# Reciprocal roots in two VectorE steps in PSUM, and the heads' rotation after their root

## The chip, the cores and the metric

The kernel runs on one core of a Trainium2 chip. The metric is the device time of one execution in microseconds, the median of several runs; lower is better.

The core has a matrix engine (TensorE, in the profile PE for its matmuls and PEld for its weight loads), an elementwise engine (VectorE, DVE), an engine for functions (ScalarE, ACT), a general engine (GpSimd, POOL) and a queue that issues transfers (SyncE, SP). Tensors lie in SBUF or in PSUM, where TensorE writes its products. Each engine works through its own instructions in a fixed order and waits for semaphores of the others.

## What is computed

The reference runs two transformer blocks, each of two layers, on 512 tokens with 1024 features, in float32. The first block mixes tokens in three ways (a Fourier transform, a gated recurrence, a latent attention) and also reads a context of 256 tokens. The second block has a grouped attention of 8 query heads over 2 key heads and a dilated attention of 3 groups of 4 heads. Every layer ends in an MLP with a squared ReLU. What matters here are the reciprocal roots, in every norm, and the norm and rotation of the heads in the second block:

```python
def rms(x, g):
    x32 = x.astype(jnp.float32)
    y = x32 * lax.rsqrt(jnp.mean(x32 * x32, axis=-1, keepdims=True) + EPS)
    return (y * g.astype(jnp.float32)).astype(x.dtype)

def apply_rope_2(x, cos, sin):
    x1, x2 = jnp.split(x32, 2, axis=-1)
    return jnp.concatenate([x1 * c - x2 * s, x2 * c + x1 * s], axis=-1).astype(x.dtype)

# for each group of the dilated attention, and in the same way for the grouped one
qs.append(apply_rope_2(rms(qb, q_norm_b[l, g]), *seq_cs))
kss.append(apply_rope_2(rms(kb, k_norm_b[l, g]), *seq_cs))
```

## The kernel before

Features lie on the partitions and tokens on the free axis, so the stream x is eight tiles of 128 x 512. Products take float32 operands in two parts, a high and a low one: a unit of weights (8 tiles of 128 x 128) is fetched by SyncE's queue, cut into its parts by ScalarE (line 120) and GpSimd (line 121), and used in 24 matmuls of 512 columns (lines 143, 144 and 146; `mm3`). TensorE runs one unit after the other through all stages, and the other engines serve it.

The program is written as Python loops and generators, which interleave their steps (`weave`); a planner then orders the instructions of each engine by their place in the program and by its own estimate of when each can start, and adds the semaphores. So the order on an engine is not exactly that of the text, and it is fixed before the run.

`rsqrt` (lines 152 to 161) makes (scale * mean + eps) ** -0.5 of a sum in PSUM. ScalarE takes a logarithm (line 156) and an exponential (line 157); then a Newton step follows on VectorE in four instructions (lines 158 to 161): one reads the sum from PSUM, three work in SBUF. It is called 64 times in an execution: by the norms of the stream (`norm_r`), by the latents' norms (`rms_small`), by the recurrence's output (`mlstm_out`) and 34 times, on 128 x 512, by `head_block`.

`head_block` (lines 1119 to 1146) takes a unit's product, the queries or keys of two heads, and normalizes and rotates it. ScalarE copies the product out of PSUM and squares it (lines 1127 to 1129), VectorE makes the low part of the squares (line 1130). The rest waits in a list, `pending`, until the next unit of products has been issued (`flush` in `project`): TensorE sums the squares over each head into a `pt` bank of PSUM (lines 1134 and 1135), `rsqrt` makes the root, and VectorE shuffles the block (line 1139), multiplies with the gains and the sine or cosine tables (lines 1140 and 1141), adds (line 1142) and multiplies with the root (line 1143). PSUM has two `pt` banks; the transposes of the attentions' softmax (lines 1184 and 1232), the value blocks and the norms take from the same two.

`mixers2` (line 1252) runs the second block's attention: a key block, four query blocks (`qa`), a `flush`, and then the six blocks of `dil_proj(0)` woven with the grouped attention (`gqa`) and the six of `dil_proj(1)` woven with the first half of the dilated attention (`dilated`). In the first layer the first block's final norm is woven in too (`finish`).

Of the kernel before, what the change touches and what calls it, by code (L numbers as in the profile page):

```python
# [10 lines left out]
F32 = mybir.dt.float32  # L11
# [6 lines left out]
EPS = 1e-6  # L18
# [5 lines left out]
HALVES = (slice(0, 256), slice(256, 512))  # L24


class Cols:
    """Per-feature vectors, side by side as columns of one array."""
# [33 lines left out]
def cut(t, H, classes):  # L62
    """The tokens H of t, whose order may be that of the classes modulo 4."""
    return by_classes(t)[:, :, H.start // 4:H.stop // 4] if classes else t[:, H]


def weave(a, b, na, nb):
    """Steps of two generators, in turn: nb of b spread over na of a."""
# [12 lines left out]
class Stream:  # L81
    """Tokens whose features lie on the partitions: x, eight blocks of [128, n]."""
# [6 lines left out]
class Kernel:  # L89
# [33 lines left out]
    def weights(self, src, nk, nm=128, dve=False, extra=None):  # L123
        """A unit of the weights, in two parts; extra: the tag of a third place."""
# [11 lines left out]
    def mm3(self, out, w, xs, ks=None, wide=False):  # L136
        """out += w[:, i].T @ xs[i], each operand in two parts."""
# [9 lines left out]
        if not wide:  # L147
            # short products leave the low part of the weights more time
            for i, (xh, xl) in enumerate(xs):
                nc.tensor.matmul(out, lo[:, ks[i] if ks else i], xh, start=False, stop=i == n - 1)  # L150

    def rsqrt(self, out, mean_ps, scale, tmp, eps=EPS):
        """out = (scale * mean + eps) ** -0.5; the tables' result takes a Newton step to float32's accuracy."""
        nc = self.nc
        p = mean_ps.shape[0]
        nc.scalar.activation(out=out, in_=mean_ps, func=AF.Ln, scale=scale, bias=(self.eps if eps == EPS else self.eps2)[:p])
        nc.scalar.activation(out=out, in_=out, func=AF.Exp, scale=-0.5)
        nc.vector.tensor_scalar(out=tmp, in0=mean_ps, scalar1=-0.5 * scale, scalar2=-0.5 * eps, op0=ALU.mult, op1=ALU.add)
        nc.vector.tensor_tensor(out=tmp, in0=tmp, in1=out, op=ALU.mult)  # L159
        nc.vector.tensor_tensor(out=tmp, in0=tmp, in1=out, op=ALU.mult)  # L160
        nc.vector.scalar_tensor_tensor(out=out, in0=tmp, scalar=1.5, in1=out, op0=ALU.add, op1=ALU.mult)

    def sigmoid(self, out, x, t=None):
        """out = 1 / (1 + exp(-x)), with no exponential of a positive number; with t, x is read at once."""
# [49 lines left out]
    def mod_cols(self, mod, ps, bias, at, nb, nv):  # L214
        """Rows 32 q + v of the sums to columns: mod[:, v, at + nb q + b]."""
# [12 lines left out]
    def gemv_now(self, r, src, out, tag, start, stop):  # L228
        """Round r of the first modulation, for both vectors, in steps, with TensorE's four column groups."""
# [17 lines left out]
    def gemvs_now(self, mod, rounds, src, bias):  # L247
        """Up to four rounds, in one tile of sums."""
# [7 lines left out]
    def gemv_later(self, mod, r, src, bias, vs):  # L256
        """A round of a modulation, in steps, on VectorE."""
# [31 lines left out]
    def until(self, n):  # L289
        """The first n of the modulations' later rounds are done."""  # L290
# [3 lines left out]
    def gain(self, name, g, sc):  # L294
        a = self.const.tile([128, 8], F32, name=name)
        self.nc.vector.scalar_tensor_tensor(out=a, in0=sc, scalar=1.0, in1=g, op0=ALU.add, op1=ALU.mult)
        return a

# [1 line left out]
    def norm_tag(self, s, H):  # L300
        """Where the tiles of a norm lie: by halves, some are held for long, and have a place of their own."""
# [4 lines left out]
    def norm_add(self, s, k, w=None, H=None):  # L306
        """Takes block k of s.x into the sum of squares, weighted with a column of w; H: of some tokens."""
# [33 lines left out]
    def scaled(self, out, x, a, r, classes):  # L341
        """out = a r x; classes: the tokens of out lie in classes modulo 4."""
# [14 lines left out]
    def norm_mod(self, s, a, sh, r=None, classes=False):  # L357
        """The normed and modulated blocks of s.x, each in two parts."""
# [20 lines left out]
    def norm_steps(self, s, a, sh, weighted=False, classes=False):  # L379
        """norm_mod by halves of the tokens; the first half's norm_r is done."""  # L380
# [1293 lines left out]
```

## Time and profile before

Three runs took 3576.43, 3580.7 and 3587.28 us; their median is 3580.7 us. The page and every row below are of one profiled execution, of which the page gives the span, from the first instruction to the last.

| | us | share of the span |
|---|---|---|
| span of the profiled execution | 3586.3 | |
| TensorE matmuls busy | 3376.2 | 94% |
| TensorE weight loads busy (beside the matmuls) | 2646.2 | 74% |
| VectorE busy | 2140.4 | 60% |
| ScalarE busy | 1456.4 | 41% |
| GpSimd busy | 1147.3 | 32% |

The span lies 5.6 us above the median of the runs and inside their spread. Busy shares are means over stages that differ; the second block's layers have their mixers at about 1960 to 2300 us and 2790 to 3110 us. The granted clock is the share of TensorE's full speed that it was allowed in a stretch; it has two levels, 2.4 GHz (1.00) and 1.2 GHz (0.50).

### The profile page before, as it was taken

What the parts mean: (1) busy time and instruction counts of PE and PEld (TensorE: products, weight loads), DVE (VectorE), ACT (ScalarE), POOL (GpSimd) and SP (SyncE); (2) the same over time, 40 slices, a digit from 0 to 9 for tenths busy, and PEclk for the clock granted to TensorE, in tenths of its full rate; (3) what the DMA queues carried; (4) which work ended last, traced back from release to release, by engine and by line L of the source; (5) the groups of instructions that cost most, each with busy time, mean ns of one, the idle gap of its engine ahead of it and who ended that gap; (6) DMA issues with size and microseconds to landing.
All of it is one profiled execution on the core that took longest, in us unless ns stands there. A gap on an engine that the chain in (4) does not pass through costs nothing.

```text
span 3586.3 us, 47387 instructions
## 1 busy us (share of the span) xinstructions
PE 3376.2 (94%) x18518; PEld 2646.2 (74%) x18518; DVE 2140.4 (60%) x3006; ACT 1456.4 (41%) x2551; POOL 1147.3 (32%) x539
## 2 busy tenths in 40 slices
PE   6989998999997889989998899999999899999999
PEld 4666667888886666678777656888888757788887
DVE  5764357564457863385667977466645867454333
ACT  4545444121233554343223555543223455643222
POOL 1222033222324321144443312344444312343443
PEclk8999999999999989999999999999999999999999
DMA  7731122343335422034453101224542101222232
GB/s 268 258 117 59 32 75 89 106 130 106 106 112 179 142 68 63 21 110 144 164 173 128 65 31 52 81 91 150 170 138 94 59 30 53 75 96 88 95 100 94
DMA packets 146706, 377.88 MB, mean 105 GB/s; under 512 B 16737, under 2 KB 32690, under 8 KB 146354
## 3 DMA queue, kind: packets, MB, share of 16 engines
q1 hardware_dynamic: 146482, 374.85, 31.9%
q8 instruction: 146, 2.39, 0.3%
q14 instruction: 78, 0.64, 0.1%
HBM read 363.48 MB, written 9.86 MB: 104 GB/s over the span
## 4 chain that ended last, share of the span: by engine, by line
PE 51%; DVE 10%; issue 2%; ACT 2%; DMA 0%; POOL 0%; DVEq 0%; ACTq 0%; POOLq 0%
PE pm L143 13%; PE pm L144 13%; PE pm L146 12%; PE p L968 1%; DVE y L346 1%; PE pt L1184 1%; PE p L1166 1%; PE pt L143 1%; PE pt L144 1%; PE pm L938 1%; PE pt L1192 1%; DVE hraw L1141 1%; PE pt L1232 1%; DVE hv L159 1%; PE pm L150 1%
## 5 line engine op out<-in xcount | busy, mean ns | idle before, releaser
L121 POOL TENSOR_TENSOR wlo<-raw,whi 128x1024 fp32r<-128x1024 f32 (+2 forms) x461 | 1096.7, 2380 | 2260.7 <-ACT whi L120 2118.7
L120 ACT CAST whi<-raw 128x1024 fp32r<-128x1024 f32 (+2 forms) x468 | 477.0, 1019 | 1208.5 <-PE pm L144 987.5
L143 PE MATMUL pm<-h,whi 128*128 128x512 f32 (+1 forms) x2312 | 856.0, 379 | 9.8 <-ACT raw_s L541 3.9
L144 PE MATMUL pm<-h,whi 128*128 128x512 f32 (+1 forms) x2312 | 844.7, 373 | 0.7 <-DVE h L374 0.7
L146 PE MATMUL pm<-h,wlo 128*128 128x512 f32 x1816 | 722.4, 398 | 3.3 <-POOL wlo L121 3.3
L143 PEld LDWEIGHTS pm<-h,whi 128*128 128x128 f32 x2312 | 443.3, 192 | 104.7 <-issue 19.0
L144 PEld LDWEIGHTS pm<-h,whi 128*128 128x128 f32 x2312 | 441.9, 191 | 77.0 <-issue 5.7
L143 PE MATMUL pm<-hid,whi 128*128 128x512 f32 (+1 forms) x1280 | 462.2, 370 | 21.8 <-DVE x L445 17.5
L144 PE MATMUL pm<-hid,whi 128*128 128x512 f32 (+1 forms) x1280 | 459.9, 368 | 3.9 <-DVE hid L513 3.9
L269 DVE SCALAR_TENSOR_TENSOR ga<-g,svec,ga 128x512 f32<-128x512 f32 x280 | 337.2, 1211 | 151.5 <-DMA g<-in_w_mod 149.9
L146 PEld LDWEIGHTS pm<-h,wlo 128*128 128x128 f32 x1816 | 346.8, 191 | 80.1 <-POOL wlo L121 5.8
L146 PE MATMUL pm<-hid,wlo 128*128 128x512 f32 x976 | 384.6, 394 | 1.7 <-POOL wlo L121 1.7
L509 DVE TENSOR_TENSOR relu<-relu 128x512 f32<-128x512 f32 (+1 forms) x169 | 255.6, 1513 | 190.1 <-ACT relu L507 189.9
L445 DVE SCALAR_TENSOR_TENSOR x<-pm,mod,x 128x512 f32<-128x512 f32 (+1 forms) x184 | 125.3, 684 | 357.9 <-PE pm L146 349.4
L143 PEld LDWEIGHTS pm<-hid,whi 128*128 128x128 f32 x1280 | 244.2, 191 | 65.7 <-issue 19.6
L144 PEld LDWEIGHTS pm<-hid,whi 128*128 128x128 f32 x1280 | 243.9, 191 | 45.4 <-DVE hid L513 6.9
L146 PEld LDWEIGHTS pm<-hid,wlo 128*128 128x128 f32 x976 | 185.6, 190 | 41.5 <-POOL wlo L121 3.0
L507 ACT ACTIVATE relu<-pm 128x512 f32<-128x512 f32 (+1 forms) x160 | 85.5, 534 | 144.9 <-PE pm L146 135.7
L513 DVE TENSOR_TENSOR hid<-relu,hid 128x512 fp32r<-128x512 f32 (+1 forms) x169 | 110.1, 651 | 14.5 <-ACT hid L512 0.4
L951 ACT ACTIVATE D<-pt,cc 128x256 f32<-128x256 f32 (+1 forms) x176 | 75.0, 448 | 99.5 <-PE pt L945 59.2
L325 DVE TENSOR_TENSOR acc<-acc,sq 128x256 f32<-128x256 f32 (+1 forms) x96 | 86.7, 903 | 25.2 <-ACT sq L317 22.7
L373 ACT ACTIVATE h<-y,mod 128x256 fp32r<-128x256 f32 (+1 forms) x136 | 67.7, 528 | 81.9 <-DVE y L346 81.6
(398 smaller groups left out, 4898.6 us busy)
## 6 DMA issues: line engine op xcount, KB each, us to landing
g<-in_w_mod SPq DMA_DIRECT2D x352, 256.0 KB, 3.0
raw<-in_w_in SPq DMA_DIRECT2D x142, 512.0 KB, 3.5
raw<-in_w_down SPq DMA_DIRECT2D x136, 512.0 KB, 3.5
raw<-in_w_up SPq DMA_DIRECT2D x128, 512.0 KB, 3.5
raw<-in_w_out SPq DMA_DIRECT2D x24, 512.0 KB, 3.5
g<-in_w_mod SPq DMA_DIRECT2D x16, 512.0 KB, 7.5
raw<-in_w_out SPq DMA_DIRECT2D x16, 384.0 KB, 3.3
raw<-in_w_br SPq DMA_DIRECT2D x16, 384.0 KB, 3.0
```

The costliest lines, as they stand in the source:

```text
L120: nc.scalar.copy(out=hi, in_=src)
L121: (eng or nc.vector).tensor_tensor(out=lo, in0=src, in1=hi.bitcast(F32), op=ALU.subtract)
L143: nc.tensor.matmul(out, hi[:, k], xh, start=i == 0, stop=False)
L144: nc.tensor.matmul(out, hi[:, k], xl, start=False, stop=False)
L146: nc.tensor.matmul(out, lo[:, k], xh, start=False, stop=i == n - 1)
L269: nc.vector.scalar_tensor_tensor(out=a, in0=g, scalar=sk, in1=a, op0=ALU.mult, op1=ALU.add)
L325: nc.vector.tensor_tensor(out=acc, in0=acc, in1=sq, op=ALU.add)
L445: nc.vector.scalar_tensor_tensor(out=x, in0=ps, scalar=ga[:, m:m + 1], in1=x, op0=ALU.mult, op1=ALU.add)
L507: nc.scalar.activation(out=r, in_=ps, func=AF.Relu)
L509: nc.vector.tensor_tensor(out=q, in0=r, in1=r, op=ALU.mult)
L513: nc.vector.tensor_tensor(out=lo, in0=q, in1=hi.bitcast(F32), op=ALU.subtract)
L951: nc.scalar.activation(out=D[:, kk, T], in_=rp[:, kk, T], func=AF.Exp, bias=cc[:, 2 * p + kk, r:r + 1])
```

## The change

`rsqrt` leaves the exponential in `tmp`, and ScalarE squares it (a third step). VectorE then has two steps: (sum + eps / scale) times the square, written over the sum in PSUM, and that minus 3 / scale, times the exponential. The result is the root times -2 / scale; the missing factor goes into the gains of all users (`NORM` in `gain`, and `times`, `gq` and `hg`).

`head_block` lets the second step write to PSUM too. VectorE multiplies the block with the root first, in SBUF, then shuffles; the sine product is written to PSUM, the cosine product to SBUF, and the sum of the two is the last step.

In `mixers2` the `flush` after the four query blocks is dropped, so the last query block's second part is issued after the next unit's products. Comments and docstrings are left out as well. The diff, cut to its core:

```diff
+NORM = -0.5 / 1024
...
-    def rsqrt(self, out, mean_ps, scale, tmp, eps=EPS):
+    def rsqrt(self, out, mean_ps, scale, tmp, eps=EPS, sq=None):
...
-        nc.scalar.activation(out=out, in_=mean_ps, func=AF.Ln, scale=scale, bias=(self.eps if eps == EPS else self.eps2)[:p])
-        nc.scalar.activation(out=out, in_=out, func=AF.Exp, scale=-0.5)
-        nc.vector.tensor_scalar(out=tmp, in0=mean_ps, scalar1=-0.5 * scale, scalar2=-0.5 * eps, op0=ALU.mult, op1=ALU.add)
-        nc.vector.tensor_tensor(out=tmp, in0=tmp, in1=out, op=ALU.mult)
-        nc.vector.tensor_tensor(out=tmp, in0=tmp, in1=out, op=ALU.mult)
-        nc.vector.scalar_tensor_tensor(out=out, in0=tmp, scalar=1.5, in1=out, op0=ALU.add, op1=ALU.mult)
+        nc.scalar.activation(out=tmp, in_=mean_ps, func=AF.Ln, scale=scale, bias=(self.eps if eps == EPS else self.eps2)[:p])
+        nc.scalar.activation(out=tmp, in_=tmp, func=AF.Exp, scale=-0.5)
+        sq = out if sq is None else sq
+        nc.scalar.activation(out=sq, in_=tmp, func=AF.Square)
+        nc.vector.scalar_tensor_tensor(out=mean_ps, in0=mean_ps, scalar=eps / scale, in1=sq, op0=ALU.add, op1=ALU.mult)
+        nc.vector.scalar_tensor_tensor(out=out, in0=mean_ps, scalar=-3.0 / scale, in1=tmp, op0=ALU.add, op1=ALU.mult)
...
         self.nc.vector.scalar_tensor_tensor(out=a, in0=sc, scalar=1.0, in1=g, op0=ALU.add, op1=ALU.mult)
+        self.nc.vector.tensor_scalar(out=a, in0=a, scalar1=NORM, scalar2=None, op0=ALU.mult)
         return a
...
+    def times(self, name, g, c):
+        t = self.const.tile([128, g.shape[-1]], F32, name=name)
+        self.nc.vector.tensor_scalar(out=t, in0=g, scalar1=c, scalar2=None, op0=ALU.mult)
+        return t
...
-            self.rsqrt(r, pr, 1.0 / 64, self.new("m", [128, 512], "hv"))
+            v = self.new("m", [128, 512], "hv")
+            self.rsqrt(pr, pr, 1.0 / 64, v, sq=r)
             g = self.hg[:, 16 * l + 2 * kind:16 * l + 2 * kind + 2]
+            nc.vector.tensor_tensor(out=raw, in0=pr, in1=raw, op=ALU.mult)
             nc.vector.stream_shuffle(out, raw, SWAP16)
-            nc.vector.scalar_tensor_tensor(out=out, in0=out, scalar=g[:, 1:2], in1=self.rope2[:, tab, 1], op0=ALU.mult, op1=ALU.mult)
+            nc.vector.scalar_tensor_tensor(out=pr, in0=out, scalar=g[:, 1:2], in1=self.rope2[:, tab, 1], op0=ALU.mult, op1=ALU.mult)
             nc.vector.scalar_tensor_tensor(out=raw, in0=raw, scalar=g[:, 0:1], in1=self.rope2[:, tab, 0], op0=ALU.mult, op1=ALU.mult)
-            nc.vector.tensor_tensor(out=raw, in0=raw, in1=out, op=ALU.add)
-            nc.vector.tensor_tensor(out=out, in0=raw, in1=r, op=ALU.mult)
+            nc.vector.tensor_tensor(out=out, in0=pr, in1=raw, op=ALU.add)
...
         qa = [self.head_block(some[2 + i] if 2 + i < SKEWED else all_(proj(2 + i)), l, 0, 0) for i in range(4)]
-        self.flush()
```

## Rows read from the trace of the kernel before

**Rows 1.** The page: busy us, share of the span and instructions of each engine.
```profile
PE 3376.2 (94%) x18518; PEld 2646.2 (74%) x18518; DVE 2140.4 (60%) x3006; ACT 1456.4 (41%) x2551; POOL 1147.3 (32%) x539
```
**Rows 2.** By stretch: us; PE, PEld, DVE, ACT, POOL busy; PE clock, DMA, GB/s.
```profile
1977.00:2016.00 39.00, 31.81 (x129) 23.39 (x128) 38.42 (x56) 19.59 (x31) 13.65 (x5) 0.95 0.22 74
2016.00:2080.00 64.00, 58.18 (x262) 41.51 (x260) 63.18 (x96) 34.69 (x66) 15.37 (x6) 0.95 0.14 49
2080.00:2220.00 140.00, 134.26 (x674) 88.58 (x675) 99.28 (x190) 78.11 (x159) 23.75 (x10) 0.96 0.12 38
2800.00:2839.00 39.00, 33.95 (x141) 25.45 (x141) 36.65 (x58) 19.70 (x31) 13.64 (x6) 0.96 0.21 70
2839.00:2910.00 71.00, 60.50 (x274) 43.62 (x273) 58.88 (x94) 35.44 (x69) 19.18 (x8) 0.93 0.18 60
```
**Rows 3.** TensorE's waits (us, times, longest) in 1977:2016, 2016:2080 and 2080:2220.
```profile
PE pt L1135 <- DVE hsq L1130: 7.2, 3, 3.3
...
PE pt L333 <- DVE acc L325: 3.1, 1, 3.1
...
PE p L1166 <- ACT P L1172: 3.7, 1, 3.7
```
**Rows 4.** The same in 2800:2839, 2839:2910 (two lines) and 2910:3040.
```profile
PE pt L1135 <- DVE hsq L1130: 5.1, 2, 2.7
...
PE pt L1184 <- DVE P L1176: 7.8, 3, 4.9
PE pt L1184 <- DVE hv L158: 2.1, 1, 2.1
...
PE pt L1232 <- DVE hv L158: 1.3, 1, 1.3
```
**Rows 5.** In order of time: start us, us, instruction [idle before, what ended it].
```profile
1972.46 2.77 DVE L1142 TENSOR_TENSOR hraw<-hraw,qk 128x512 f32<-128x512 f32 x1
...
1985.23 2.44 POOL L121 TENSOR_TENSOR wlo<-raw,whi 128x1024 fp32r<-128x1024 f32 x1 [4.63 <-ACT whi L120]
...
1985.34 2.89 DVE L1141 SCALAR_TENSOR_TENSOR hraw<-hraw,hg,rope 128x512 f32<-128x512 f32 x1
...
1989.35 0.68 DVE L161 SCALAR_TENSOR_TENSOR hr<-hv,hr 128x512 f32<-128x512 f32 x1
1989.95 0.68 DVE L1130 TENSOR_TENSOR hsq<-qk,hsq 128x512 fp32r<-128x512 f32 x1
...
1990.69 0.50 PE L1135 MATMUL pt<-hsq,bd64r 128*128 128x512 f32 x1 [2.37 <-DVE hsq L1130]
```
**Rows 6.** Groups by line, 1977:2220: count | busy us, mean ns of one | idle before.
```profile
L159 DVE TENSOR_TENSOR hv<-hv,hr 128x512 f32<-128x512 f32 x17 | 16.3, 960 | 0.6 <-ACT hr L157 0.6
L161 DVE SCALAR_TENSOR_TENSOR hr<-hv,hr 128x512 f32<-128x512 f32 x17 | 13.8, 813 | 0.1
...
L158 DVE TENSOR_SCALAR hv<-pt 128x512 f32<-128x512 f32 x17 | 11.6, 681 | 11.8 <-ACT hr L156 11.8
```
**Rows 7.** Line 955 over the whole span: ns of one, min/median/max, first and last start.
```profile
L955 DVE TENSOR_TENSOR W<-pm,D x48: 677/692/693, 383.2 to 1513.5; 128x512 f32<-128x512 f32 x48
```
**Rows 8.** By stretch, as rows 2, behind the stall of rows 5.
```profile
1991.80:1995.20 3.40, 3.40 (x10) 2.62 (x9) 3.40 (x7) 2.13 (x5) 0.00 (x0) 0.51 0.00 0
```
**Rows 9.** In order of time: a root of the latents' norm, VectorE not crowded.
```profile
1239.19 0.69 ACT L156 ACTIVATE r_s<-pt,eps 128x512 f32<-128x512 f32 x1 [2.93 <-PE pt L548]
...
1240.71 0.69 DVE L159 TENSOR_TENSOR v_s<-v_s,r_s 128x512 f32<-128x512 f32 x1
...
1242.89 0.75 DVE L553 SCALAR_TENSOR_TENSOR raw_s<-raw_s,gq1x,r_s 128x512 f32<-128x512 f32 x1
```
**Rows 10.** In order of time: the end of a head block, and transposes behind it.
```profile
2209.57 0.68 DVE L158 TENSOR_SCALAR hv<-pt 128x512 f32<-128x512 f32 x1
...
2210.31 0.66 PE L1232 MATMUL pt<-ident,Pd 128*128 128x128 f32 x4 [1.64 <-DVE hv L158]
...
2212.77 0.68 DVE L1143 TENSOR_TENSOR qk<-hraw,hr 128x512 f32<-128x512 f32 x1
```

More of the change, by code (lines that the diff above doesn't have):

```diff
@@ L579, in latents @@
         ps = self.project(src[1], hs, n)
-        o["kv"] = self.rms_small(s, [ps], [self.col(f"gkv{l}")], 1.0 / 128, "Wc" if "Wc" in self.bufs else "so" if "so" in self.bufs else "W")
+        o["kv"] = self.rms_small(s, [ps], [self.times(f"gkv{l}{s.name}", self.col(f"gkv{l}"), -0.5 / 128)], 1.0 / 128, "Wc" if "Wc" in self.bufs else "so" if "so" in self.bufs else "W")
         kA = []
@@ L591, in latents @@
             gq = self.const.tile([128, 2], F32, name=f"gq{l}{s.name}")
-            nc.vector.tensor_scalar(out=gq, in0=self.col(f"gq{l}", 0, 2), scalar1=96.0 ** -0.5, scalar2=None, op0=ALU.mult)
+            nc.vector.tensor_scalar(out=gq, in0=self.col(f"gq{l}", 0, 2), scalar1=-0.5 / 256 * 96.0 ** -0.5, scalar2=None, op0=ALU.mult)
             o["q"] = self.rms_small(s, pq, [gq[:, i:i + 1] for i in range(2)], 1.0 / 256, "ya" if "so" in self.bufs else "W")
@@ L912, in mlstm @@
         rows, cc, negm = rows_cc
+        o["gm"] = self.times(f"gm{l}{s.name}", self.col(f"gm{l}", 0, 3), -0.5 / 96)
         VM, qk = o["VM"], o["qk"]
@@ L1017, in mlstm_out @@
         for j in range(3):
-            nc.vector.scalar_tensor_tensor(out=sq[:, j], in0=H0[:, j], scalar=self.col(f"gm{l}", j), in1=r, op0=ALU.mult, op1=ALU.mult)
+            nc.vector.scalar_tensor_tensor(out=sq[:, j], in0=H0[:, j], scalar=o["gm"][:, j:j + 1], in1=r, op0=ALU.mult, op1=ALU.mult)
             self.put_y(s, ys, 2 + j, sq[:, j], cQ)
@@ L1150, in head_gains @@
         self.hg = self.const.tile([128, 32], F32, name="hg")
-        nc.vector.tensor_copy(out=self.hg, in_=self.col("hgain", 0, 32))
+        nc.vector.tensor_scalar(out=self.hg, in0=self.col("hgain", 0, 32), scalar1=-0.5 / 64, scalar2=None, op0=ALU.mult)
         q = self.hg.rearrange("p (l t g) -> p l t g", l=2, g=4)[:, :, :, 0:2]
@@ L1472, in finish @@
                             r = K.norm_r(X)
+                            gr = K.times("gr", gf, NORM)
                             for k in range(8):
-                                K.scaled(X.x[k], X.x[k], gf[:, k:k + 1], r, False)
+                                K.scaled(X.x[k], X.x[k], gr[:, k:k + 1], r, False)
                                 yield True
```

## The prediction

> **What bounds the kernel now.** I read the page's busy times first [rows 1]: TensorE is busy 94% of the span, VectorE 60%. A change that touches VectorE and ScalarE alone can win only where TensorE stands still or runs at the lower clock, so the next view is the table by stretch [rows 2], cut at the five stages that hold the head blocks (17 in each of the second block's two layers, 34 in all). I call the first five head blocks of a layer stage A (1977 to 2016, 2800 to 2839), the next six, woven with the grouped attention, stage B (2016 to 2080, 2839 to 2910), and the last six, woven with the dilated attention, stage C. The reader is to see that in A and in the first layer's B VectorE is busy for 38.42 of 39 and 63.18 of 64 us, while TensorE is not: there VectorE is the bound, inside a kernel that is TensorE's elsewhere. In C VectorE has 99.28 of 140 us and TensorE 134.26: TensorE's stretch.
>
> Third, TensorE's own waits in these stretches [rows 3, 4]. In A all of them are line 1135 waiting for line 1130: 7.2 us in the first layer, 5.1 in the second. Line 1130 makes the low part of a block's squares; it is not slow, it stands in VectorE's queue behind the root and rotation steps of the block before. In B the waits are the softmax's scaling, a sum of the final norm, and one wait for line 158, which is a wait for a bank of PSUM.
>
> Fourth, the order of time in one such stall [rows 5]. GpSimd starts its weight split at 1985.23; VectorE starts line 1141 at 1985.34, and it takes 2.89 us. Line 1130 starts at 1989.95, and TensorE resumes at 1990.69 after 2.37 us. Line 159, two inputs in SBUF, has a mean of 960 ns in the first layer, where its undisturbed neighbours take 0.68; line 158, which reads PSUM, has 681 [rows 6], and line 955, one input in PSUM and one in SBUF, never took more than 693 ns in 48 [rows 7]. So it is the steps with two inputs in SBUF that GpSimd holds up. After the stall TensorE is granted 0.51 of its clock for 3.4 us, its level of 1.2 GHz [rows 8]; so a stall costs more than its length.
>
> **The change, part by part.**
>
> *Head blocks, VectorE's steps.* Before, a block has ten steps: 1130, 158 to 161, 1139 to 1143. After, eight: 1130, two for the root, the product with the block, the shuffle, the two rotation products, the sum. Adjacent steps start 0.60 us apart (1989.35 to 1989.95) [rows 5], so two fewer are 1.2 us a block. Of steps with two SBUF inputs eight become three (1130 and the two rotation products). The excess of lines 159 and 161 alone over 0.68 us is 0.960 + 0.813 - 2 x 0.68 = 0.41 us a block [rows 6]. Not all of it goes: a GpSimd step that no longer meets line 159 can meet one of the three that stay. Between 0 and 0.41 I take 0.3, since the share of steps that can be hit falls from 8 in 10 to 3 in 8. Together 1.5 us a block.
>
> The new steps write to PSUM, which no VectorE row here does. From below 0: no row with an operand in PSUM is shorter than its neighbours in SBUF (681 and 692 against 0.68). From above 0.07 us each, the dearest undisturbed step of this size being line 553 with 0.75 [rows 9]: 0.2 us a block in three writing steps, 7 us over 34 blocks. I take 0, the nearest rows being lines 158 and 955 [rows 6, 7]. A rule speaks against this: the Trainium skill (Perfetto Trace Analysis, Optimizing Scalar/DVE Operations) gives a VectorE step an overhead of about 60 ns in SBUF and about 125 in PSUM. By that figure the four more steps that touch PSUM would cost an estimated 0.26 us a block, and the sum below would be about 3 us smaller. The trace does not show the difference: 681 ns against 0.68 us.
>
> *ScalarE.* One Square more for each of the 64 roots, 0.69 us at 512 columns by line 156 [rows 9]. In A and B ScalarE has 19.59 of 39 and 34.69 of 64 us [rows 2], so its time is covered; if ScalarE were full, 12 blocks a layer would cost 12 x 0.69 = 8 us.
>
> *Latency of one root.* Where VectorE is not crowded, line 156 starts at 1239.19, line 159 at 1240.71 and the user at 1242.89 [rows 9]: two ScalarE steps of 0.76 and three dependent VectorE steps of 0.73 make 3.70 us. After: three and two, 3.74. So the small norms and the norms of the stream gain nothing in an empty queue, and up to two steps in a crowded one. I count -1 us for all of them, with ends at -5 and +1. The gains' extra products are 64 columns or less, outside any stall: 0.
>
> *The rotation.* Before, lines 1139 to 1142 need no root and can run ahead of it; now all seven steps wait for it. Behind the waiting step on VectorE stand the next block's line 1130 and the softmax; behind those, TensorE. In a full queue other work is there to fill. The first block of a layer loses its head start: before, four of its steps ran ahead of stage A (its line 1142 starts at 1972.46) [rows 5]; now seven instead of five come after the sum, +1.2 us.
>
> *PSUM's two `pt` banks.* A block's bank was free after line 158; now it is held to the block's last step. In the block shown [rows 10] line 158 ends at 2210.25 and the last step, line 1143, at 2213.45: 3.2 us more, less the two steps saved (1.2): 2 us.
>
> *The dropped flush (line 1266).* It moves the fifth block's last part behind the next unit of weights. TensorE's order is already a planner's, which puts other matmuls between lines 1134 and 1135, so I count 0; the stall it aims at is inside the A waits below, and at most 1.5 us a layer would be its own.
>
> **The sum.** A: four blocks x 1.5 - 1.2 = 4.8 us of VectorE's time a layer; TensorE's waits there are 7.2 and 5.1 us, and the low clock costs 39 x 0.05 = 2.0 and 39 x 0.04 = 1.6, so there is room: -4.8 x 2 = -9.6. B: six blocks x 1.5 = 9 us a layer, but the waits for softmax and norm also hang on ScalarE; room is 3.1 + 3.7 + 64 x 0.05 = 10.0 and 7.8 + 2.1 + 71 x 0.07 = 14.9. I take half of VectorE's saving, -4.5 x 2 = -9. C: VectorE's time is worth nothing; one `pt` wait a layer grows by 2: +4. Norms: -1. In all -15.6 us. The profiled execution's span is 3586.3, which would become 3570.7; it lies 5.6 us above the median of the runs, 3580.7, and inside their spread. From the median: **3565 us**.
>
> **The rivals.**
>
> *More: every stall of A and B goes, with its clock.* The caps add up to 9.2 + 6.7 + 10.0 + 14.9 = 40.8 us: 3540. For it: the three stalls of A are the chain itself. Against: TensorE's order is fixed ahead by the planner, so some steps will again be placed too early. Somewhere near 3545; chance 0.10.
>
> *Same: what VectorE saves goes into waiting for ScalarE.* The root now needs three ScalarE steps before VectorE's first; in rows 9 that is 0.76 more, with nothing of the block's own left to fill it. If a block loses that, 1.5 becomes 0.74, A and B give 9 instead of 18.6, C takes 4 of it: 3575. For it: in an empty queue the chain begins with ScalarE's steps already [rows 9]. Against: in a full queue it has other work. Chance 0.28; here belongs the case that the planner's new order costs about as much as it saves.
>
> *Slower: the two `pt` banks become the bound.* Transposes of both attentions, the value blocks and the roots all take from these two. Of 24 blocks in B and C, three now show a wait on line 158 that stops TensorE: 2.1 and 1.3 us [rows 4] and 1.64 [rows 10]. Where TensorE has a unit of products ready it passes the wait; where a transpose is next it stops. Each stop costs 2 to 3 us; A and B gain 18.6, so past 18.6 / 2.5 = 7 to 8 stops the change loses. With 12, half of the blocks: 3580.7 + 12 x 2.5 - 18.6 = 3592. For it: the hold grows on every block. Against: 21 of 24 blocks now stop nobody. Chance 0.17.
>
> **How the numbers follow.** The forecast has 0.45: 3551 to 3570 around 3565. With "more", faster by over 0.3% (about what a measurement of this kernel can tell from no change, 10.7 us) has 0.55; same has 0.28; slower 0.17. The range reaches from the caps, 3540, to a little above the slower rival, 3596; it leaves out the tails of both. It takes in the price of writing PSUM (7 us) and the roots' ends.
>
> **What would show it.** Right: VectorE has two fewer steps a block; its two root steps and the last sum stay near 0.69 us with GpSimd running; TensorE's waits on line 1130 in A fall from 12.3 us to under 4; the A stretches shorten by about 5 us each and the low clock in them with it. Wrong: root steps of 0.75 or more; waits of transposes (lines 1184, 1232) on a block's last sum that add up to over 10 us; VectorE idle behind the Square in A; stalls that only move, with A as long as before; or a changed order that costs time in stages where nothing was edited, which this sum cannot see.

## The result, and the profile after

Four runs of the changed kernel took 3538.78 to 3551.0 us, median **3543.9**; the kernel before, beside them, had a median of 3581.8. The ratio is 0.9887, 95% interval 0.9866 to 0.9909: 38 us faster. The forecast was 3565, 16 us faster, so the sign and the range held and the size did not. The profiled execution of after has a span of 3537.0 us, 49.3 less than that of before; one is near the low end of its runs, the other near the high end, so some 11 of the 49 us are the choice of execution.

The page of after (busy us, share of the span, instructions), for [rows 1]:

```profile
PE 3362.9 (95%) x18518; PEld 2636.5 (75%) x18518; DVE 2036.5 (58%) x2897; ACT 1490.4 (42%) x2615; POOL 1142.1 (32%) x539
```

VectorE has 109 instructions and 104 us less, ScalarE 64 squares and 34 us more. TensorE does the same work in a shorter span.

**Where the time went.** The first logarithm of a head block marks the start of each of the second block's layers. Before, these two lay at 1978.01 and 2803.51 us. The first two lines are of after, the other two of a second profile of the same kernel (run e9 below):

```profile
1958.36 0.69 ACT L158 ACTIVATE hv<-pt,eps 128x512 f32<-128x512 f32 x1
2767.00 0.68 ACT L158 ACTIVATE hv<-pt,eps 128x512 f32<-128x512 f32 x1
```
```profile
1972.98 0.68 ACT L158 ACTIVATE hv<-pt,eps 128x512 f32<-128x512 f32 x1
2781.54 0.68 ACT L158 ACTIVATE hv<-pt,eps 128x512 f32<-128x512 f32 x1
```

From mark to mark a layer took 825.5 us before and 808.64 after, and in the second profile 808.56. The second layer to the end of the span (3586.3, 3537.0 and 3550.3) took 782.8, 770.0 and 768.8. So the second block repeats within 1.3 us and gained 30 us in both profiles. What lies ahead of it moved by 19.7 us in one and 5.0 in the other: it differs by 15 us between two executions of one kernel, and has to be judged by medians.

The head stages by stretch, for [rows 2] (us; PE, PEld, DVE, ACT, POOL busy; granted clock, DMA share, GB/s), first A, B and C of the first layer, then A and B of the second:

```profile
1957.00:1988.00 31.00, 28.72 (x126) 21.65 (x125) 27.66 (x46) 22.93 (x38) 11.98 (x5) 1.00 0.24 77
1988.00:2047.00 59.00, 54.70 (x259) 38.53 (x258) 52.92 (x87) 39.09 (x74) 14.75 (x6) 1.00 0.18 63
2047.00:2183.00 136.00, 132.55 (x681) 88.52 (x679) 84.82 (x174) 81.58 (x161) 23.80 (x10) 0.99 0.12 39
2764.00:2796.00 32.00, 29.75 (x130) 22.52 (x128) 27.02 (x45) 22.36 (x36) 11.74 (x5) 1.00 0.25 82
2796.00:2864.00 68.00, 59.15 (x278) 42.78 (x278) 52.11 (x84) 38.04 (x75) 16.96 (x8) 0.95 0.19 62
```

VectorE was busy for 38.42 of 39 us in A; it is now for 27.66 of 31. The clock of 0.93 to 0.96 is 0.99 or 1.00 but for the second layer's B. Measured by the logarithms of the head blocks, from a layer's first to its sixth (A), from there to the eleventh, B's last, and from there to the next layer or the end, A is shorter by 8.7 and 6.6 us in the two layers, B by 4.6 and 2.6, C and what follows by 3.6 and 3.5.

TensorE's waits in these stages (us in total, times, longest), of after, 1957:2183 and then 2764:3001:

```profile
PE pt L1195 <- DVE P L1187: 3.6, 2, 1.9
PE pt L702 <- DVE qk L1154: 3.4, 1, 3.4
PE pt L1144 <- DVE qk L1154: 2.3, 2, 1.9
PE pm L147 <- POOL wlo L122: 0.5, 1, 0.5
PE pt L342 <- DVE acc L334: 0.2, 1, 0.2
...
PE pt L1195 <- DVE qk L1154: 5.0, 2, 3.3
PE pt L702 <- DVE qk L1154: 3.8, 2, 3.4
PE pt L1144 <- DVE qk L1154: 2.2, 2, 1.9
```

The wait for the low part of the squares, line 1130 before and 1140 now, is gone from [rows 3, 4]. What is left ends for the most part in **line 1154, a block's last step**: the matmul is one that takes a `pt` bank (a sum, a transpose, a value block), and the bank comes free with that step. The same listing of before, 1977:2220 and 2800:3040, adds up to 18.6 and 18.7 us; that of after to 10.0 and 11.0. So 16 of the 30 us are waits. The granted clock accounts for most of the rest: length times missing share, over A to C of both layers, is 18.6 us before and 6.1 after.

How such a wait looks in order of time (start, us, instruction, idle before and what ended it):

```profile
1984.90 0.68 DVE L1154 TENSOR_TENSOR qk<-pt,hraw 128x512 f32<-128x512 f32 x1
1985.23 2.37 POOL L122 TENSOR_TENSOR wlo<-raw,whi 128x1024 fp32r<-128x1024 f32 x1 [3.51 <-ACT whi L121]
1985.50 0.69 DVE L163 SCALAR_TENSOR_TENSOR pt<-pt,hv 128x512 f32<-128x512 f32 x1
...
1985.72 0.47 PE L1144 MATMUL pt<-hsq,bd64r 128*128 128x512 f32 x1 [0.42 <-DVE qk L1154]
```

A block's last step ends at 1985.58 and the next block's sum takes the bank at 1985.72. It also shows a root step (line 163) of 0.69 us that begins while GpSimd works. This wait is one of the short ones, 0.42 us. The longest of the first layer has more behind it:

```profile
2049.77 2.40 POOL L122 TENSOR_TENSOR wlo<-raw,whi 128x1024 fp32r<-128x1024 f32 x1 [5.82 <-ACT whi L121]
2049.86 2.85 DVE L1153 SCALAR_TENSOR_TENSOR hraw<-hraw,hg,rope 128x512 f32<-128x512 f32 x1
...
2052.74 0.69 DVE L1154 TENSOR_TENSOR qk<-pt,hraw 128x512 f32<-128x512 f32 x1
...
2053.58 0.63 PE L702 MATMUL pt<-ident,vt 128*128 128x128 f32 x4 [3.44 <-DVE qk L1154]
```

The cosine product (line 1153), which has two inputs in SBUF, began 0.09 us after GpSimd's split and took 2.85 us, where its undisturbed time is 0.75; the last step came that much later. All five waits of 1.9 to 3.4 us on line 1154, 13.9 of its 16.7 us, stand behind a rotation product (line 1152 or 1153) of 2.84 to 2.86 us that began within 0.11 us of a split. With 0.75 us in its place these five waits would be some 10 us shorter, an estimate: two by their whole 1.86 us, three by 2.1. So a large part of what is left is the old hold-up by GpSimd, which now reaches TensorE through the bank instead of through the low part of the squares.

VectorE's groups by line in 1957:2183 (count | busy us, mean ns of one | idle before), for [rows 6]:

```profile
L1152 DVE SCALAR_TENSOR_TENSOR pt<-qk,hg,rope 128x512 f32<-128x512 f32 x17 | 14.9, 877 | 0.2
L1153 DVE SCALAR_TENSOR_TENSOR hraw<-hraw,hg,rope 128x512 f32<-128x512 f32 x17 | 14.7, 867 | 0.0
L1140 DVE TENSOR_TENSOR hsq<-qk,hsq 128x512 fp32r<-128x512 f32 x16 | 14.1, 884 | 11.0 <-PE pt L1144 9.5 <-ACT hsq L1139 1.3
...
L162 DVE SCALAR_TENSOR_TENSOR pt<-pt,hr 128x512 f32<-128x512 f32 x17 | 11.8, 694 | 16.5 <-ACT hr L161 16.4
L163 DVE SCALAR_TENSOR_TENSOR pt<-pt,hv 128x512 f32<-128x512 f32 x17 | 11.8, 694 | 0.2
L1150 DVE TENSOR_TENSOR hraw<-pt,hraw 128x512 f32<-128x512 f32 x17 | 11.6, 684 | 0.1
L1154 DVE TENSOR_TENSOR qk<-pt,hraw 128x512 f32<-128x512 f32 x17 | 11.6, 683 | 0.1
```

The four steps that read PSUM take 683 to 694 ns, whether they write to it or not. The three that have two inputs in SBUF have means of 867 to 884, and so has line 1152 among them, which writes to PSUM: it is the inputs that count. VectorE stands idle for the Square (line 161) for 16.4 us here, 4.6 more than it stood for line 156 before (11.8, rows 6).

### The profile page after: what moved, and what is told of

The parts are those of the page before. It is cut to its first block, busy times and chain, and to the rows that moved or that the text cites. A ratio compares the mean times of both kernels' runs of the same rounds, so it can differ in the third digit from the quotient of the medians.

```text
span 3537.0 us, 47303 instructions
## 1 busy us (share of the span) xinstructions
PE 3362.9 (95%) x18518; PEld 2636.5 (75%) x18518; DVE 2036.5 (58%) x2897; ACT 1490.4 (42%) x2615; POOL 1142.1 (32%) x539
## 4 chain that ended last, share of the span: by engine, by line
PE 55%; DVE 7%; ACT 2%; issue 1%; DMA 0%; POOL 0%; DVEq 0%; ACTq 0%; POOLq 0%
PE pm L144 14%; PE pm L145 14%; PE pm L147 13%; PE p L978 1%; PE p L1177 1%; DVE y L355 1%; PE p L1222 1%; PE pt L1195 1%; PE pt L1203 1%; PE pt L144 1%; PE pt L1243 1%; PE pt L145 1%; PE pm L948 1%; PE pm L151 1%; PE pt L147 1%
## 5 line engine op out<-in xcount | busy, mean ns | idle before, releaser
L144 PEld LDWEIGHTS pm<-h,whi 128*128 128x128 f32 x2312 | 442.0, 191 | 103.2 <-issue 19.7
L522 DVE TENSOR_TENSOR hid<-relu,hid 128x512 fp32r<-128x512 f32 (+1 forms) x169 | 111.9, 662 | 14.9 <-DVE relu L518 0.5
```

The costliest lines, as they stand in the source:

```text
L144: nc.tensor.matmul(out, hi[:, k], xh, start=i == 0, stop=False)
L522: nc.vector.tensor_tensor(out=lo, in0=q, in1=hi.bitcast(F32), op=ALU.subtract)
```

## The experiments

Each ran beside the kernel before on the same chip. "us" is the difference of the medians (kernels of different chips are compared by it); the third column is the second block's two layers in the profiled execution, mark to end, against before's 1608.3 us.

| run | what | ratio to before, 95% interval | us | second block, us |
|---|---|---|---|---|
| e1 | new root in the 30 small roots alone | 0.9976 (0.9964 to 0.9988) | -8.7 | +3.4 |
| e2 | new root and rotation in the 34 head blocks alone | 0.9920 (0.9901 to 0.9938) | -27.8 | -29.0 |
| e3 | flush dropped alone | 0.9996 (0.9983 to 1.001) | -0.5 | -1.0 |
| e4 | the change, all results in SBUF | 0.9941 (0.9924 to 0.9959) | -20.9 | -7.5 |
| e5 | before, Newton steps in PSUM | 0.9922 (0.9907 to 0.9936) | -27.1 | -13.4 |
| e6 | before, bank held to the block's end | 1.0005 (0.9988 to 1.0023) | +2.7 | +5.3 |
| e7 | the change, rotation ahead of the root | 0.9923 (0.9907 to 0.9938) | -26.4 | -12.5 |
| e8 | the change, two more products in PSUM | 0.9908 (0.9892 to 0.9923) | -30.7 | -17.8 |
| e9 | the change again | 0.9888 (0.9870 to 0.9907) | -37.0 | -30.9 |
| e10 | the change, one more ScalarE step in the chain | 0.9946 (0.9930 to 0.9962) | -18.0 | -7.0 |
| e11 | the change, two more VectorE steps a head | 0.9920 (0.9905 to 0.9936) | -25.9 | -17.2 |
| e12 | the change, two more VectorE steps a small root | 0.9893 (0.9877 to 0.9909) | -37.6 | -25.5 |
| e13 | the change, no Square, three VectorE steps | 0.9950 (0.9935 to 0.9966) | -17.4 | -9.8 |
| e14 | the change, sine product in SBUF | 0.9931 (0.9909 to 0.9953) | -24.5 | -21.3 |
| e15 | the change, one more ScalarE step beside the chain | 0.9889 (0.9864 to 0.9914) | -38.2 | -27.7 |

The planner orders the instructions anew for every kernel. Three edits that should cost nothing (e3, e12, e15) came out within 0.1% of the kernel that they were made to, but their second block moved by up to 5 us; differences of that size in the last column carry nothing.

**The parts alone.** e1 keeps the four-step root in `head_block`, e2 keeps it everywhere else, e3 drops one line:

```diff
 # e1: in head_block, of before otherwise
-            self.rsqrt(r, pr, 1.0 / 64, self.new("m", [128, 512], "hv"))
+            self.rsqrt_4(r, pr, 1.0 / 64, self.new("m", [128, 512], "hv"))
 # e2: in head_block, of after otherwise
-            self.rsqrt(pr, pr, 1.0 / 64, v, sq=r)
+            self.rsqrt_2(pr, pr, 1.0 / 64, v, sq=r)
 # e3: in mixers2
-        self.flush()
```

> The new root in the norms of the stream, the latents and the recurrence's output alone (30 of the 64); head blocks and the flush as before. The step theory (each part pays by the VectorE steps that it takes out of a crowded queue, and the parts add up to the 38 us): 8 to 15 us faster than before, 3567 to 3574, since the changed kernel's profile is 19 us ahead when the first block ends, of which some is scatter between executions. The order theory (the first block's gain is the planner's new order and scatter, as an empty queue gives 3.74 us for 3.70): within 4 us of before, 3578 to 3586.

> The new root and rotation in the 34 head blocks alone; the other roots and the flush as before. Step theory: 20 to 26 us faster than before, 3556 to 3562, with the head stages of the profile 12 to 15 us shorter in each layer. Flush theory (most of the head stages' gain comes from the dropped flush, since both layers gain 6 us at the fifth block): 10 to 14 us faster, 3568 to 3572, and waits on line 1130's successor stay at the fifth block. Order theory: 35 us or more, so that the other parts give nothing.

> The kernel before without the flush after the four query blocks. Step theory: 0 to 3 us faster, 3579 to 3582, as the stall at line 1135 is VectorE's lateness and not TensorE's order. Flush theory: 10 to 14 us faster, 3568 to 3572, 5 to 7 in each layer at the fifth block.

-8.7, -27.8 and -0.5 us add up to -37.0, what the whole gives. The flush is worth nothing, as the prediction had it. The second block's gain is that of the heads (e2, -29.0). The small roots give 9 us, and their profile shows no gain in the second block: it lies in the first.

**Count or placement.** e4 makes every step of the change, but writes root, product and rotation to SBUF, as the kernel before does; e5 leaves all ten steps and only places the Newton steps in PSUM:

```diff
 # e4
-        nc.vector.scalar_tensor_tensor(out=mean_ps, in0=mean_ps, scalar=eps / scale, in1=sq, ...)
+        nc.vector.scalar_tensor_tensor(out=sq, in0=mean_ps, scalar=eps / scale, in1=sq, ...)
...
-            nc.vector.scalar_tensor_tensor(out=pr, in0=out, scalar=g[:, 1:2], ...)
+            nc.vector.scalar_tensor_tensor(out=out, in0=out, scalar=g[:, 1:2], ...)
 # e5, of the kernel before
-        nc.vector.tensor_scalar(out=tmp, in0=mean_ps, ...)
-        nc.vector.tensor_tensor(out=tmp, in0=tmp, in1=out, op=ALU.mult)
+        nc.vector.tensor_scalar(out=mean_ps, in0=mean_ps, ...)
+        nc.vector.tensor_tensor(out=mean_ps, in0=mean_ps, in1=out, op=ALU.mult)
```

> The changed kernel with the same number of steps in the same order, but the root's first step, the root, the head's sine product and its sum in SBUF: steps with two inputs in SBUF are six of eight instead of three, and the bank of PSUM is free after the root's first step. Step theory with GpSimd's hold-ups: 8 to 15 us slower than the changed kernel, 3552 to 3559, with means of the two-input steps at 800 to 1000 ns. Rival (the count of steps alone pays, the place of the operands is nothing): within 4 us of the changed kernel, 3540 to 3548. Bank theory (the longer hold of the bank costs): faster than the changed kernel, below 3540.

> The kernel before with its ten VectorE steps a head block and its four Newton steps a root, but each of the first three now writes over the sum in PSUM, so that no root step has two inputs in SBUF. Number of steps, order of the rotation and length of the bank's hold stay. Theory of contention (steps with two inputs in SBUF are held up while GpSimd works, those with one in PSUM are not): the excess of lines 159 to 161 (12 us in the profile before) goes, the head stages win 8 to 15 us, the first block about 0. Rival, that only the number of steps counts: within 3 us of before. Rival, that a write to PSUM costs more than one to SBUF: 64 roots x 3 steps x up to 0.07 us, 0 to 10 us slower.

The change's steps with their results in SBUF give 21 us, placement alone 27, both 37. Line 159 of the heads before (first fence), and the steps of e5's heads, over the whole span:

```profile
L159 DVE TENSOR_TENSOR hv<-hv,hr 128x512 f32<-128x512 f32 x34 | 30.4, 895 | 1.3 <-ACT hr L157 1.3
```
```profile
L1141 DVE SCALAR_TENSOR_TENSOR hraw<-hraw,hg,rope 128x512 f32<-128x512 f32 x34 | 41.5, 1222 | 0.0
L1142 DVE TENSOR_TENSOR hraw<-hraw,qk 128x512 f32<-128x512 f32 x34 | 31.4, 925 | 0.4
L159 DVE TENSOR_TENSOR pt<-pt,hr 128x512 f32<-128x512 f32 x34 | 23.5, 690 | 1.2 <-ACT hr L157 1.2
L160 DVE TENSOR_TENSOR pt<-pt,hr 128x512 f32<-128x512 f32 x34 | 23.5, 690 | 0.1
```

Line 159, 895 ns before, is at 690 with its operands moved and nothing else; the rotation's steps, left in SBUF, stay at 925 and 1222. The expectation named 8 to 15 us in the head stages, and 13.4 came; it named 0 for the first block, and that was a miss: the medians differ by 27.1, twice what the second block shows.

e4 is not the count of steps alone. Let the excess be the time that VectorE's 512-column head steps take, over all 34 blocks, above their undisturbed 0.685 us (0.75 for those with a gain and for the shuffle). It is 46.8 us before, 31.1 in e5, 31.5 in e4 and 18.3 in the change: e4 lost hold-ups as well, so what two steps fewer are worth by themselves is not isolated. Nor is it the number of exposed steps alone that counts. In e4 the root's last step, the product and the last sum have two inputs in SBUF again, yet means of 685 and 686 ns; what is held up more is the two rotation products, 1221 and 1057 ns against 941 and 929 in the change, with their inputs in SBUF in both. It counts too which step is due when GpSimd begins.

**Why the first block gained.** The small roots' last step before (first fence) and after, over the whole span:

```profile
L161 DVE SCALAR_TENSOR_TENSOR r<-v,r 128x512 f32<-128x512 f32 x3 | 4.2, 1386 | 0.1
L161 DVE SCALAR_TENSOR_TENSOR r_s<-v_s,r_s 128x256 f32<-128x256 f32 x3 | 2.5, 826 | 0.0
```
```profile
L163 DVE SCALAR_TENSOR_TENSOR r<-pt,v 128x512 f32<-128x512 f32 x3 | 2.1, 689 | 0.1
```

A few steps were held up (1386 ns as a mean of three, the longest 2776) and none is now. e12 asks whether the count of steps counts too:

```diff
 # e12: in rsqrt, for all roots but the heads'
+            for _ in range(2):
+                nc.vector.tensor_scalar(out=mean_ps, in0=mean_ps, scalar1=1.0, scalar2=None, op0=ALU.mult)
```

> The changed kernel with two more VectorE steps, multiplications by one in place in PSUM, in each of the 30 roots that are not the heads': 23 of 256 columns (0.43 us a step) and 7 of 512 (0.69 us), 2 x (23 x 0.43 + 7 x 0.69) = 29 us of VectorE's time, most of it in the first block. Theory that these roots stand on the path with TensorE behind them, by their steps: 10 to 25 us slower than the change. The prediction's view (they win nothing by count): within 3 us. Theory that the first block's gain came from the three exposed steps alone that were held up to 2.8 us in the profile before: within 3 us too.

With 29 us more of VectorE's time it is as fast as the change, 0.9893 against 0.9888. So the count is worth nothing there, as the prediction said; the gain that it missed is the one of e1, and e5, which has no step fewer, gained ahead of the second block too. That the held steps are its whole cause is argued, not shown: in the profile of before they add up to 5 us only.

**The bank.** e6 lengthens the hold at the old count and order:

```diff
 # e6, of the kernel before: the root's last step writes to pr (last=pr), and
-            nc.vector.tensor_tensor(out=out, in0=raw, in1=r, op=ALU.mult)
+            nc.vector.tensor_tensor(out=out, in0=pr, in1=raw, op=ALU.mult)
```

> The kernel before, with one change: the root's last step writes to the block's own bank of PSUM and the last product reads it there, so that the bank is held to the block's end instead of to line 158 (seven steps of 0.68 us at most, some 3 to 4 us longer), while number and order of the steps stay. Theory that the two banks are the bound in the grouped and dilated stages (the rival that would have made the change slower, and the +4 us of the prediction's stage C): 4 to 30 us slower, with waits of the transposes on a block's last step. Theory that the banks have slack: within 4 us of before.

Nothing measurable in time. Its profile does show waits for the last step (line 1143), 9.8 us in the two layers (1976:2230 and 2812:3050); but all of TensorE's waits there add up to 37.8 us, against 37.3 before. So they took the place of other waits. e10 and e15 add the same ScalarE step to the changed kernel, e10 inside the chain from the sum to the last step, e15 beside it:

```diff
 # e10: in rsqrt, of the heads, ahead of the Square
+            nc.scalar.copy(out=tmp, in_=tmp)
 # e15: in head_block, behind rsqrt
+            nc.scalar.copy(out=lo, in_=r)
```

> The changed kernel itself, beside the three that follow, as their measure: 0.9887 of before, within 0.002.

> The changed kernel with one more ScalarE step (a copy in place, 0.7 us at 512 columns) between the exponential and the square of each of the 34 heads' roots: twice the delay that the new Square brought. The rival of the prediction, that the steps saved go into waiting for ScalarE: 0.7 us for most of the 22 blocks of stages A and B, 10 to 16 us slower than the change. The theory that other work fills VectorE's queue meanwhile: within 3 us of the change.

> The changed kernel with one more ScalarE step in each of the 34 heads' roots, as in the run that was 19 us slower, but beside the chain: it copies the square into a tile that nobody reads any more (0.65 us), after the Square, and VectorE does not wait for it. ScalarE's time is the same as in that run. If the delay of the chain made the 19 us: within 5 us of the change. If ScalarE's queue made them (the softmax's exponentials stand behind): 10 to 20 us slower than the change.

ScalarE's time beside the chain is free (0.9889), in the chain it costs 19 us (18.0 won instead of 37.0), 0.56 for each of 34 blocks. So it is not ScalarE's fill. The waits of e10 in 2070:2220 and 2880:3030, where the change has none but one of 3.4, show whom the delay meets:

```profile
PE pt L1245 <- DVE qk L1156: 3.2, 1, 3.2
PE pt L704 <- DVE qk L1156: 1.1, 1, 1.1
...
PE pt L704 <- DVE qk L1156: 5.1, 2, 4.0
PE pt L1245 <- DVE qk L1156: 3.1, 1, 3.1
```

Line 1156 is the block's last step there, 1245 the transposes of the dilated attention, which waited for no block in the change. But a chain that starts later also changes which step GpSimd meets. The cosine product of e10, and that of the change (second fence), over the whole span:

```profile
L1155 DVE SCALAR_TENSOR_TENSOR hraw<-hraw,hg,rope 128x512 f32<-128x512 f32 x34 | 48.6, 1428 | 0.0
```
```profile
L1153 DVE SCALAR_TENSOR_TENSOR hraw<-hraw,hg,rope 128x512 f32<-128x512 f32 x34 | 31.6, 929 | 0.0
```

Each of the five waits above stands behind a cosine product of 2.84 or 2.85 us. The excess of e10 is 29.5 us, that of the change 18.3, that of e15 14.9. So e10 shows what the delay cost in this kernel, hold-ups included; that a longer hold of the bank costs time by itself is not shown.

**Steps of the heads.** e11 adds two steps that GpSimd does not hold up; e13 takes the Square away for a third VectorE step:

```diff
 # e11: in head_block, ahead of the product with the root
+            for _ in range(2):
+                nc.vector.tensor_scalar(out=pr, in0=pr, scalar1=1.0, scalar2=None, op0=ALU.mult)
 # e13: in rsqrt
-        nc.scalar.activation(out=sq, in_=tmp, func=AF.Square)
-        nc.vector.scalar_tensor_tensor(out=mean_ps, in0=mean_ps, scalar=eps / scale, in1=sq, ...)
+        nc.vector.scalar_tensor_tensor(out=mean_ps, in0=mean_ps, scalar=eps / scale, in1=tmp, ...)
+        nc.vector.tensor_tensor(out=mean_ps, in0=mean_ps, in1=tmp, op=ALU.mult)
```

> The changed kernel with two more VectorE steps a head block, multiplications by one in place in PSUM, which GpSimd does not hold up: the number of steps of before (ten) without its exposed ones. Pure count, as the prediction had it: 1.2 to 1.4 us for each of the 22 blocks of stages A and B where VectorE is the bound, 5 in the second A and first A less one each, 10 to 25 us slower than the change. If the gain came from the exposed steps alone: within 5 us of the change.

> The changed kernel with no Square on ScalarE: VectorE multiplies the sum twice with the exponential, in place in PSUM, so a root has two ScalarE steps and three VectorE steps (0.69 us each at 512 columns, none with two inputs in SBUF). A head block has nine steps. The run with one more ScalarE step in each head root was 19 us slower than the change, that with two more VectorE steps 11 us. If ScalarE's queue is what counts there: -19 + 11 / 2, about 13 us faster than the change, 0.985 of before. If the delay from the sum to the root is what counts: it stays as it is (0.65 against 0.69 us), and one VectorE step costs: 0 to 6 us slower than the change, 0.989 to 0.9905. The prediction's view (ScalarE covered, VectorE the bound in A and B): 6 us slower.

Two steps cost 11 us, 0.33 a block, within what was expected. It is not the count alone either: e11's sine product (line 1154) has a mean of 1261 ns, against 941 in the change, and its excess is 27.0 us. These waits of e11, in 1960:2210, are again those of banks:

```profile
PE pt L1245 <- DVE qk L1156: 4.9, 2, 3.3
PE pt L1144 <- DVE qk L1156: 2.3, 3, 1.2
```

e13 lost 20 us against the change, more than any theory gave it, with a delay like the change's and one step fewer than e11. In 1970:2230 its sums alone wait for line 1153, its last step, 7.0 us:

```profile
PE pt L1143 <- DVE qk L1153: 7.0, 3, 3.1
PE pt L701 <- DVE qk L1153: 4.4, 2, 3.1
PE pt L1194 <- DVE qk L1153: 3.4, 1, 3.4
```

All five waits of the first two lines stand behind a cosine product (line 1152) of 2.84 to 2.88 us; its mean over the run is 1244 ns, against 929 in the change, and e13's excess is 31.1 us. So in these waits the bank is late behind a step that GpSimd held up. Why it meets that step more often in e13 stays open; the planner ordered each kernel anew.

**Where the rotation's results should lie.** e7 puts the rotation ahead of the root, e8 takes two more steps into PSUM, e14 takes the rotation out of it:

```diff
 # e7
+            nc.vector.stream_shuffle(out, raw, SWAP16)
+            ... (both products and the sum in SBUF)
+            nc.vector.tensor_tensor(out=out, in0=pr, in1=raw, op=ALU.mult)
 # e8: product with the root and cosine product to pr, sine product to out
-            nc.vector.tensor_tensor(out=raw, in0=pr, in1=raw, op=ALU.mult)
+            nc.vector.tensor_tensor(out=pr, in0=pr, in1=raw, op=ALU.mult)
 # e14
-            nc.vector.scalar_tensor_tensor(out=pr, in0=out, scalar=g[:, 1:2], ...)
+            nc.vector.scalar_tensor_tensor(out=out, in0=out, scalar=g[:, 1:2], ...)
```

> The changed kernel with its two-step root in PSUM, but the rotation ahead of the root as before: shuffle, sine product, cosine product and sum in SBUF, then the product with the root read from PSUM. Eight steps as in the change; five have an operand in PSUM in the change, three here; the low part and three rotation steps have two inputs in SBUF, against three steps in the change. Contention theory: one more exposed step a block, 34 x 0.1 to 0.2 us, and a few us of TensorE's waits with it: 3 to 10 us slower than the change, 0.990 to 0.992 of before. Rival, that the rotation's head start is worth its price (the prediction charged 1.2 us a layer and a wait for ScalarE): 2 to 15 us faster than the change.

> The changed kernel with the product of block and root, and the cosine product, written in place to PSUM too; the shuffle reads PSUM and the sine product goes to SBUF. Eight steps as in the change, and only the low part and the sine product have both inputs in SBUF (three in the change). Contention theory: the cosine product's excess (6 us over the run) goes, some 2 to 6 us faster than the change, ratio to before about 0.987. Rival, that what is left of the contention costs TensorE nothing any more: the same as the change within 2 us. If a shuffle from PSUM is dear (no run has shown one): slower than the change.

> The changed kernel with the root and the product with it in PSUM as they are, but the sine product in SBUF: the bank is free two or three steps earlier (1.5 to 2.2 us), and the last sum has two inputs in SBUF too (four exposed steps of eight instead of three). The kernel with everything in SBUF stood 0.0054 behind the change. If the hold of the bank costs: faster than the change by up to 10 us. If the exposed steps cost: slower by 5 to 12 us. Which of the two placements the 20 us belong to: the root's (then this run lies within 4 us of the change) or the rotation's (then it lies within 6 us of 0.9941).

e7 is 11 us behind the change, as the contention theory had it, in spite of the head start. e8 was expected ahead of the change and is not: 0.9908 against 0.9888, with intervals that overlap. Its cosine product, with one input in PSUM, is held up no more (a mean of 742 ns), but its sine product is instead (1116 ns, 941 in the change). e14 lies between e4 and the change. It frees its banks earlier, and indeed no wait for a block's last step is left in 1958:2220; others have come back:

```profile
PE pt L1145 <- DVE hsq L1140: 3.6, 1, 3.6
PE p L1177 <- ACT P L1183: 3.5, 1, 3.5
```

These are those of [rows 3, 4]: the low part and the softmax behind a crowded VectorE. In the second block e4, e14 and the change win 7.5, 21 and 30 us, as more results move to PSUM; the medians of e4 and e14 are too near to each other to tell them apart (0.9941 and 0.9931). No version that was tried beats the change.

**The hold-ups of all runs.** The excess of the heads orders the profiles. It is 45 to 49 us before and in e1, e3 and e6, whose second block lies within 6 us of before; 27 to 32 in e4, e5, e7, e10, e11, e13 and e14, which win 7 to 21 us there; and 15 to 18 in the change and in e2, e8, e9, e12 and e15, which win 18 to 31. With one profile each this is an order and not a price, and what differs inside a group is not explained by it.

## Why the prediction was right in sign and wrong in size

Three terms of the sum failed: stage C, the small roots, and the contention in the heads, which stands in A and B. In the sum's own terms, A measured -15.3 us for -9.6, B -7.2 for -9, C and what follows -7.1 for +4, and the small roots -8.7 (e1) for -1. Together that is -38.3, and the result is 38.

That the time lies at the place of the rival "more" (near 3545, chance 0.10) is luck: that rival takes 40.8 us out of A and B, which gave 22.5.

**What bounds the kernel** held. In the second block TensorE gained where it had stood or run slowly, and the waits on line 1130, 12.3 us of A, fell to nothing, as the list of signs asked. It failed for **stage C**, of which the prediction said that VectorE's time is worth nothing there. C's waits before were softmax steps and banks behind VectorE's queue; that of after is one of 3.4 us, at the border of B and C. And its clock had room: 140 us at 0.96 [rows 2] lack 5.6 us, 136 at 0.99 lack 1.4.

**The held bank** failed twice. As a cost it was counted from one block's arithmetic, 2 us more for one wait a layer; e6 shows that a hold to the block's end cost nothing measurable. As a rival it named the right place: all of the second layer's remaining waits and over half of the first's are for a block's last step. But the price was taken for stops that add to the old waits, and they replaced them instead; and behind most of their length stands a rotation product that GpSimd held up, which the rival did not have.

**The small roots** were sized at -1 with an end at -5, and e1 measured -8.7. Their latency was read in an empty queue [rows 9], and "up to two steps in a crowded one" counted steps; a step that GpSimd holds up for 2 us was not looked for outside the heads.

**Contention in the heads** was undersized: 0.3 us a block. The excess of 46.8 us before and 18.3 after is 28 us less, 0.84 a block. The bound of 0.41 was worked out from lines 159 and 161 alone, while the rotation's lines 1141 and 1142, which [rows 5] show at 2.89 and 2.77 us, carried 25 of the 46.8. The two steps saved came, but no run shows the 1.2 us that they were to be worth: two steps more cost 0.33 a block in e11, hold-ups included. In A TensorE gained more than forecast; in B less, and there waits for the banks took some back. The reading that steps with two inputs in SBUF are those that GpSimd holds up left one kind out: the softmax's scaling (line 1176 before), with one tensor read there, took up to 2.58 us in place of 0.48.

**PSUM's price** of 0 was right. The Trainium skill (Perfetto Trace Analysis, Optimizing Scalar/DVE Operations) would make each step with PSUM an estimated 65 ns dearer; the trace has 683 to 694 ns against a median of 680 for line 1143 before, in SBUF, so it does not show that. By the sum's own weights that rule would have made the forecast smaller by 3.6 us rather than 3.

**The rival of ScalarE** (0.28) did not happen, but e10 shows that it was near: 0.6 us more in each chain takes half of the gain. It is not ScalarE's fill that does it, which is free (e15). In e10 the later chain came with 11 us more of hold-ups and with waits for the bank; what the delay would cost without them is open. VectorE's idle time behind the Square in A, one of the prediction's signs of being wrong, is 2.1 us a layer. And the rival's sum is rough: with 0.74 a block and the 1.2 for the head start, A and B give 8.0, not 9, which changes no chance.

## What to carry to other kernels

Count what a VectorE step costs from all of its neighbours' means while GpSimd runs, not from one line: with one input moved from SBUF to PSUM the same step fell from 895 to 690 ns. When VectorE's queue gets shorter, look for what is late next by tile name, and then for what stood before it: here TensorE's new waits are for two banks of PSUM, but behind most of their length stands a step that GpSimd held up. Before a slower run is put down to the step that was added to it, compare the means of the steps that were not touched: a delay also changes which of them GpSimd meets (929 ns in the change, 1428 in e10). And take a gain apart by stretches only where two executions of the same kernel agree: here the second block repeated within 1.3 us and the first differed by 15.

## What the runs showed of the hardware

Over the whole of before the longest head step with two inputs in SBUF took 2.93 us, beside a GpSimd split of 2.4; of the changed kernel's root steps, products and last sums in PSUM none took over 0.72 us. The Trainium skill (SBUF — State Buffer, Who interferes with whom) states it so: a VectorE instruction with at most one input in SBUF does not contend with GpSimd, outside the 2-port performance modes, and one with two does when GpSimd reads SBUF. For these steps the trace agrees. One input in SBUF does not spare every step: the softmax's scaling (line 1187 after), which reads one tensor there, has a median of 0.48 us and took up to 2.63, beside a split of 2.75; whether that is the page's exception no run here tests. Not expected was that the gain of placement and that of the change's steps in SBUF do not add (27 and 21 us alone, 37 together). In the excess they nearly do: 15.7 and 15.3 us less alone, 28.5 together.

The low clock followed the waits: in A of the first layer the granted clock was 0.95 with 7.2 us of waits, and is 1.00 with 2.3. So 12.5 us of the second block's gain stand in the clock, beside 16 in the waits themselves.
